# One low part of a weight form in each second pair: a subtraction on VectorE instead of an accumulating DMA

## The chip, the cores and the metric

The kernel runs on one core of one Trainium2 chip. The metric is the device time of one execution in microseconds; lower is better. A core has TensorE for matrix products, VectorE (DVE in the profile) and ScalarE (ACT) for elementwise work, GpSimd (POOL) and SyncE (SP), and 16 DMA engines that all queues share.

## The reference

A two-layer encoder over 512 frames of 1024 features. Layer 0 mixes with an mLSTM, layer 1 with a gated MLP; each layer is wrapped by two half-step SwiGLU feed-forward networks and ends with a gated embedding. The change lies in the feed-forward network, which is run four times:

```python
def swiglu_ffn(x, w_gu, w_d):
    g, u = jnp.split(x @ w_gu, 2, axis=-1)
    return (jax.nn.silu(g) * u) @ w_d
...
    x = layer_norm(DN_ALPHA * x + 0.5 * swiglu_ffn(x, ffn1_wgu[i], ffn1_wd[i]), ln_g[i, 0], ln_b[i, 0])
```

x is 512 x 1024, w_gu 1024 x 5632 and w_d 2816 x 1024, all in float32.

## The kernel before, in words

**Split operands.** A float32 product is made of three matmuls on parts of reduced precision: high by high, low by high, high by low (lines 387 to 389). So every weight tile becomes two tiles before TensorE may use it: the high part, `whi`, a copy on ScalarE (line 274), and the low part, `wlo`, which is the tile minus its high part.

**Two ways to make a low part.** Either VectorE subtracts (line 283 at once, or line 289 later: then it stands in a list, `pending`, until `lows` is called); or ScalarE writes the negative of the tile's reduced copy into `wlo` (line 280) and GpSimd issues a DMA that adds the tile onto it (line 281). For the second way `by_dma` must hold the form.

**Seven products for eight.** The hidden width of 2816 is 22 blocks of 128, taken in chunks of 2, 4, 4, 4, 4, 4 blocks (`FFN_CHUNKS`). In the last two chunks, 4 and 5, the product that goes up, x times w_gu, is made pair by pair of blocks: gate and up columns, each in two halves of the inner dimension, are four quarters of w_gu of 128 x 1024 elements (512 KB each, loaded by SyncE into halves of three `wbox` buffers, or whole buffers of 1 MB called `wraw` once the chunk is over). From them `up_forms` builds seven forms in place, by additions and subtractions on VectorE (lines 139 and 140 for the third, 147 and 148 for the fifth), and TensorE makes seven products instead of eight. `UP_BY_DMA = (1, 3, 4, 5, 6)` says which of the seven forms, counted from 0, get their low part from a DMA; forms 0 and 2 get it from VectorE.

**Order of the work.** A chunk of four blocks has two pairs, so 14 products up, here called u0 to u13 (u0 to u6 of the first pair, u7 to u13 of the second), and seven products down for the chunk before, d0 to d6. `ffn_weights` writes the order: u0 u1 d0 u2 u3 d1 u4 u5 d2 u6 u7 d3 u8 u9 d4 u10 u11 d5 u12 u13 d6. The fifth form of the second pair, form 4 there, belongs to u11. A product up is 24 matmuls of 256 columns, one down 12 of 512 columns. Two products up and one down are called a block of work below.

**Buffers and who waits.** The high and low tiles of the products up have four buffers each (`W_BUFS`), so the form of u11 is made after u7 has been given back, while TensorE is at d3. In a step of `up_products` the order in the program is: the product's matmuls, the taking of its result, the low part of the hidden activations' form (`finish_form`, line 943, tile `flo`), the pending low parts of weights (`W.lows`, line 1143), then new forms (`W.release`). VectorE and ScalarE run strictly in that order. The form of u11 frees a quarter of w_gu when its low part is made (`done`, line 287): by DMA that is when the accumulating DMA has landed, since it reads the quarter. The next load into that place on SyncE's queue waits for it, and everything behind it on that queue too.

The tiles' names in the profile: `ups` the result of a product up, `gps` of one down, `fhi` and `flo` the parts of the hidden activations' form, `us` and `xt` partial sums, `wquarter` the quarters of w_d.

Of the kernel before, what the change touches and what calls it, by code (L numbers as in the profile page):

```python
# [17 lines left out]
P = 128  # L18
# [5 lines left out]
HID = 2816  # L24
# [19 lines left out]
EXTRA = 2  # L44
PLE_EXTRA = 3
UP_BY_DMA = (1, 3, 4, 5, 6)


class Weights:
# [75 lines left out]
        self.after.update({t2: (made[0][1],), t1: (made[1][1], t2)})  # L125
        return [(kind, js, make) for js, make in made]

    def up_forms(self, j11, j12, j21, j22):

        vec, raws = self.nc.vector, self.raws  # L130

        def a11():
            return raws[j11], ()

        def a12():
            return raws[j12], ()

        def s2():
            vec.tensor_add(raws[j21], raws[j21], raws[j22])
            vec.tensor_sub(raws[j11], raws[j21], raws[j11])  # L140
            return raws[j11], ()

        def s1():
            return raws[j21], (j21,)

        def s3():
            vec.tensor_sub(raws[j12], raws[j12], raws[j11])
            vec.tensor_sub(raws[j11], raws[j22], raws[j11])
            return raws[j11], (j11,)

        def s4():
            return raws[j12], (j12,)

        def a22():
            return raws[j22], (j22,)

        made = [((j11,), a11), ((j12,), a12), ((j21, j22), s2), ((), s1), ((), s3), ((), s4), ((), a22)]
        for _, make in made:
            self.in_place.add(make)
        self.after.update({s2: (a11,), s3: (a12, s2)})  # L160
        self.by_dma.update(made[r][1] for r in UP_BY_DMA)
        return [("main", js, make) for js, make in made]

    def spare(self, kind):
# [192 lines left out]
def hybrid_trunk(ctx: ExitStack, tc, x, p, ln_g, ln_b, ffn1_wgu, ffn1_wd, ffn2_wgu, ffn2_wd,  # L357
# [87 lines left out]
    def kp(w):  # L445
        return w.rearrange("(kb p) c -> p kb c", p=P)
# [4 lines left out]
    def add_pairs(w, a0, b0):  # L451

        W.add((w_cols(w, a0), cols2), (w_cols(w, b0), cols2))
# [4 lines left out]
    def add_rows(w, kb, n, kind="main"):  # L458
        for k in range(0, n, 2):
            W.add((kp(w)[:, kb + k:kb + k + 2, :], rows2), kind=kinds_of(kind, k))  # L460
# [14 lines left out]
    def ffn_weights(wgu, wd, name, ple=False):  # L475
        starts = [sum(FFN_CHUNKS[:c]) for c in range(LAST + 1)]

        def forms(c):
            m = FFN_CHUNKS[c] // 2

            def quarter(i, j):
                k = starts[c] + m * i
                return kp(wd)[:, k:k + m, j * 512:(j + 1) * 512]
            loads = [W.add_load(quarter(i, j), n, name) for i, j, n in ((0, 0, 2), (0, 1, 1), (1, 1, 1), (1, 0, 2))]
            return W.forms("rows", *((j, slice(None)) for j in loads))

        first = len(W.order)
        for at in range(starts[UP_FROM]):
            if at == 0 or at == starts[UP_FROM] - 1:
                W.add(*((kp(wgu)[:, :, c0:c0 + P], [slice(None)]) for c0 in (at * P, HID + at * P)))  # L490
            elif at % 2:
                add_pairs(wgu, at * P, HID + at * P)
        tiles = W.order[first:]
        del W.order[first:]
        for c, n in enumerate(FFN_CHUNKS):
            down_w = deque(forms(c - 1) if c else ())
            if c >= UP_FROM:
                products = []
                for b in range(starts[c], starts[c] + n, 2):
                    products += W.up_forms(*(W.add_load(kp(wgu)[:, k:k + 4, c0:c0 + 2 * P], 1, "box")  # L500
                                             for c0 in (b * P, HID + b * P) for k in (0, 4)))
                for s, product in enumerate(products):
                    W.order.append(product)
                    if s % 2:
                        W.order.append(down_w.popleft())
                continue
            for i in range(2 * n):
                W.order.append(tiles[2 * starts[c] + i])
                if down_w:
                    W.order.append(down_w.popleft())  # L510
        if ple:
            W.add_hook("rows", lambda hi, lo: turn_p.pop()(hi, lo))
        add_rows(wd, starts[LAST], 4, ["rowsx", "rows", "main", "main"] if ple else ["main", "rows", "rowsx", "rows"])
# [74 lines left out]
    def ple_weights(i):  # L588
        add_rows(ple_wp[i], 0, 2)
        add_wide(ple_wg[i], 0, ["extra", "extra", "extra", "main"])  # L590
        add_wide(ple_wg[i], 512, ["rows", "rows", "rowsx", "rows2"])

    ffn_weights(ffn1_wgu[0], ffn1_wd[0], (0, 0))
    ml_weights()
    ffn_weights(ffn2_wgu[0], ffn2_wd[0], (0, 2), True)
    ple_weights(0)
    ffn_weights(ffn1_wgu[1], ffn1_wd[1], (1, 0))
    gm_weights()
    ffn_weights(ffn2_wgu[1], ffn2_wd[1], (1, 2), True)
# [1350 lines left out]
```

## Time and profile before

| | |
|---|---|
| median of 3 runs | 2241.99 us (2235.75 to 2245.25) |
| the profiled execution's own time | 2245.95 us |
| its span on the core | 2244.2 us |
| mean granted TensorE clock | 0.992 |
| busy: TensorE, VectorE, ScalarE, GpSimd | 98%, 75%, 48%, 8% |
| accumulating DMAs of 512 KB from `wbox` tiles | 80 |
| HBM read | 224.58 MB, 101 GB/s over the span |

Busy shares are of the span. An engine's row in the timeline has its start, its duration, the line, the tiles as written <- read, and in square brackets how long the engine had been idle before it and what ended that. A row of the windows has the stretch, its length, then for each engine its busy time with the count of instructions, then the granted clock, the busy share of the DMA engines and their GB/s. A row of DMA issues has the number of issues, the size and the median time from issue to landing in us.

### The profile page before, as it was taken

The numbers are of one execution on the slowest core, as the hardware profiler recorded it, in microseconds if no ns is written. First come the engines' busy times: TensorE is split into PE (matmuls) and PEld (weight loads), VectorE is DVE, ScalarE is ACT, GpSimd is POOL, SyncE is SP. The second block draws the span as 40 slices with busy tenths as digits, with TensorE's granted clock in tenths as the row PEclk, the third lists the DMA queues.
The fourth block names the chain that finished last, engine by engine and source line by source line (L and its number), as shares of the span: only waits on it lengthen the run. The fifth ranks groups of instructions, "written<-read, shape, count | busy, mean of one in ns | idle before, by whom it ended". The sixth has DMA issues, their size and how long they took to land.

```text
span 2244.2 us, 29572 instructions
## 1 busy us (share of the span) xinstructions
PE 2205.9 (98%) x11669; PEld 1900.9 (85%) x11669; DVE 1675.5 (75%) x2436; ACT 1076.6 (48%) x1508; POOL 172.5 (8%) x215
## 2 busy tenths in 40 slices
PE   9999999999999999999999999999999999999998
PEld 8888988888888888888888888898888888888987
DVE  5668877786767776697786768886788767678887
ACT  3334655464646433356444334665345553336642
POOL 1000110111101100001000000110001100001100
PEclk9999999999999999999999999999999999999999
DMA  6334864456847432267632334764437743336651
GB/s 194 105 99 132 185 147 138 104 137 136 155 127 150 132 127 91 89 153 171 173 127 67 113 103 121 189 137 137 141 93 140 162 140 113 103 113 139 156 176 57
DMA packets 218355, 295.71 MB, mean 132 GB/s; under 512 B 7604, under 2 KB 162356, under 8 KB 218216
## 3 DMA queue, kind: packets, MB, share of 16 engines
q1 hardware_dynamic: 168592, 211.83, 29.3%
q0 software_dynamic: 43008, 67.30, 18.5%
q10 hardware_dynamic: 6616, 14.69, 1.9%
q8 instruction: 92, 1.51, 0.3%
q14 instruction: 47, 0.39, 0.0%
HBM read 224.58 MB, written 2.11 MB: 101 GB/s over the span
## 4 chain that ended last, share of the span: by engine, by line
PE 76%; DVE 11%; ACT 5%; DMA 4%; issue 3%; POOL 0%; SPq 0%; DVEq 0%; POOLq 0%; ACTq 0%
PE fps L387 7%; PE fps L388 7%; PE fps L389 7%; PE gps L387 5%; PE gps L388 5%; PE gps L389 5%; DMA wlo<-wbox 3%; PE dps L388 2%; PE dps L389 2%; PE dps L387 2%; DVE wlo L289 2%; PE ups L389 2%; PE ups L387 2%; PE ups L388 2%; ACT whi L274 1%
## 5 line engine op out<-in xcount | busy, mean ns | idle before, releaser
L274 ACT ACTIVATE whi<-wraw 128x1024 fp32r<-128x1024 f32 (+1 forms) x276 | 283.2, 1045 | 95.5 <-DVE wraw L118 22.5
L387 PE MATMUL fps<-xh,whi 128*128 128x512 f32 x800 | 311.4, 389 | 0.0
L388 PE MATMUL fps<-xl,whi 128*128 128x512 f32 x800 | 311.2, 389 | 0.0
L389 PE MATMUL fps<-xh,wlo 128*128 128x512 f32 x800 | 311.2, 389 | 0.0
L283 DVE TENSOR_TENSOR wlo<-wraw,whi 128x1024 fp32r<-128x1024 f32 (+1 forms) x204 | 245.0, 1215 | 48.8 <-ACT whi L274 48.0
L387 PE MATMUL gps<-whi,fhi 128*128 128x512 f32 x644 | 252.8, 393 | 0.0
L388 PE MATMUL gps<-wlo,fhi 128*128 128x512 f32 x644 | 252.3, 392 | 0.0
L389 PE MATMUL gps<-whi,flo 128*128 128x512 f32 x644 | 251.8, 391 | 0.0
L274 ACT ACTIVATE whi<-wquarter 128x1024 fp32r<-128x1024 f32 (+1 forms) x140 | 135.7, 969 | 213.1 <-PE gps L389 136.4
L283 DVE TENSOR_TENSOR wlo<-wquarter,whi 128x1024 fp32r<-128x1024 f32 (+1 forms) x92 | 97.6, 1061 | 151.9 <-ACT whi L274 151.9
L762 DVE TENSOR_TENSOR xt<-xt,gps 128x512 f32<-128x512 f32 x302 | 193.5, 679 | 5.5 <-PE gps L389 5.5
L274 ACT ACTIVATE whi<-wbox 128x1024 fp32r<-128x1024 f32 x112 | 117.9, 1052 | 131.5 <-DVE wbox L140 63.6
L389 PEld LDWEIGHTS fps<-xh,wlo 128*128 128x128 f32 x800 | 150.2, 188 | 31.5
L387 PEld LDWEIGHTS fps<-xh,whi 128*128 128x128 f32 x800 | 150.2, 188 | 31.0
L388 PEld LDWEIGHTS fps<-xl,whi 128*128 128x128 f32 x800 | 150.2, 188 | 30.9
L389 PE MATMUL ups<-xh,wlo 128*128 128x256 f32 x512 | 150.5, 294 | 22.1 <-DMA wlo<-wbox 22.1
L281 POOL DMA_DIRECT2D wlo<-wbox x80 | 68.0, 850 | 1170.6 <-ACT wlo L280 968.9
L387 PE MATMUL ups<-xh,whi 128*128 128x256 f32 x512 | 149.5, 292 | 0.4
L388 PE MATMUL ups<-xl,whi 128*128 128x256 f32 x512 | 149.0, 291 | 0.0
L389 PEld LDWEIGHTS gps<-whi,flo 128*128 128x128 f32 x644 | 121.3, 188 | 26.5
L387 PEld LDWEIGHTS gps<-whi,fhi 128*128 128x128 f32 x644 | 122.0, 189 | 24.0
L388 PEld LDWEIGHTS gps<-wlo,fhi 128*128 128x128 f32 x644 | 121.7, 189 | 23.7
(365 smaller groups left out, 5203.3 us busy)
## 6 DMA issues: line engine op xcount, KB each, us to landing
wraw<-in_ffn_wgu_dram SPq DMA_DIRECT2D x47, 1024.0 KB, 6.7
wlo<-wbox POOLq DMA_DIRECT2D x80, 512.0 KB, 5.9
wquarter<-in_ffn_wd_dram SPq DMA_DIRECT2D x64, 512.0 KB, 3.8
wbox<-in_ffn_wgu_dram SPq DMA_DIRECT2D x64, 512.0 KB, 5.5
wraw<-in_ml_w_in_dram SPq DMA_DIRECT2D x24, 1024.0 KB, 5.6
wlo<-wraw POOLq DMA_DIRECT2D x48, 512.0 KB, 6.4
wraw<-in_gm_w_in_dram SPq DMA_DIRECT2D x15, 1024.0 KB, 5.7
wraw<-in_ffn_wgu_dram SPq DMA_DIRECT2D x17, 512.0 KB, 4.9
```

The lines of the kernel that those rows point to most:

```text
L274: self.nc.scalar.activation(hi[:, s], src[:, s], AF.Copy)
L281: self.nc.gpsimd.dma_start(lo[:, s], src[:, s], accum_op=OP.add)
L283: self.nc.vector.tensor_sub(lo[:, s], src[:, s], hi[:, s].bitcast(F32))
L289: self.nc.vector.tensor_sub(lo, src, hi.bitcast(F32))
L387: mm(ps, st[0], mv[0], start=start, stop=False, skip_group_check=more)
L388: mm(ps, st[0], mv[1], start=False, stop=False, skip_group_check=more)
L389: mm(ps, st[1], mv[0], start=False, stop=stop, skip_group_check=more)
L762: vec.tensor_add(dst, dst, ps)
```

## The change

Form 4 of the second pair of each chunk leaves the set of forms whose low part is made by DMA. With four feed-forward networks, two such chunks each and one such form in each, that is eight forms in the program. For each of them ScalarE's negative copy (line 280) and GpSimd's accumulating DMA (line 281) go, and VectorE gets one subtraction of 128 x 1024 elements (line 289), through the list of pending low parts. The first pair is as before, and so is everything else.

```diff
 UP_BY_DMA = (1, 3, 4, 5, 6)
+UP_BY_DMA_2 = (1, 3, 5, 6)
...
-    def up_forms(self, j11, j12, j21, j22):
+    def up_forms(self, j11, j12, j21, j22, by_dma=UP_BY_DMA):
...
-        self.by_dma.update(made[r][1] for r in UP_BY_DMA)
+        self.by_dma.update(made[r][1] for r in by_dma)
...
                     products += W.up_forms(*(W.add_load(kp(wgu)[:, k:k + 4, c0:c0 + 2 * P], 1, "box")
-                                             for c0 in (b * P, HID + b * P) for k in (0, 4)))
+                                             for c0 in (b * P, HID + b * P) for k in (0, 4)),
+                                            by_dma=UP_BY_DMA if b == starts[c] else UP_BY_DMA_2)
```

The program's lines are one to three further down after the change (289 becomes 290). The rows below are of the first feed-forward network, chunk 4, around the form of u11; its parts are `whi_2108` and `wlo_2109`.

VectorE before, from the taking of u8's result on (`us_2106`):

```order
L1087 TENSOR_TENSOR us_2106<-us_2106,ups_2132 128x512 [waits PE_49,Activation_49]
L943 TENSOR_TENSOR flo_2130<-h_1296,fhi_2129 128x512 [waits Activation_49]
L289 TENSOR_TENSOR wlo_2127<-wquarter_1466,whi_2126 128x1024
L762 TENSOR_TENSOR xt_86<-xt_86,gps_1839 128x512 [waits DVE_49,PE_49]
L762 TENSOR_TENSOR xt_86<-xt_86,gps_1840 128x512 [waits DVE_49,PE_49]
L943 TENSOR_TENSOR flo_2219<-h_1296,fhi_2218 128x512 [waits Activation_49]
```

VectorE with the change, at the same place:

```order
L1089 TENSOR_TENSOR us_2106<-us_2106,ups_2129 128x512 [waits PE_49,Activation_49]
L945 TENSOR_TENSOR flo_2127<-h_1296,fhi_2126 128x512 [waits Activation_49]
L290 TENSOR_TENSOR wlo_2109<-wbox_1595,whi_2108 128x1024 [waits DVE_49]
L290 TENSOR_TENSOR wlo_2124<-wquarter_1466,whi_2123 128x1024
L764 TENSOR_TENSOR xt_86<-xt_86,gps_1839 128x512 [waits DVE_49,PE_49]
L764 TENSOR_TENSOR xt_86<-xt_86,gps_1840 128x512 [waits DVE_49,PE_49]
L945 TENSOR_TENSOR flo_2218<-h_1296,fhi_2217 128x512 [waits Activation_49]
```

The new subtraction stands behind `flo`, which waits for ScalarE, and ahead of the low part of d5's weights.

ScalarE before, from the high part of u11's form on:

```order
L274 ACTIVATE whi_2108<-wbox_1595 128x1024 [waits DVE_49,Activation_49]
L280 ACTIVATE wlo_2109<-wbox_1595 128x1024 [waits DMASW5_49]
L274 ACTIVATE whi_2126<-wquarter_1466 128x1024 [waits PE_49,Activation_49]
L940 ACTIVATE fhi_2129<-h_1296 128x512 [waits Activation_49]
L274 ACTIVATE whi_2164<-wbox_1595 128x1024 [waits PE_49,Activation_49]
L280 ACTIVATE wlo_2165<-wbox_1595 128x1024 [waits DMASW1_49,PE_49]
```

ScalarE with the change:

```order
L275 ACTIVATE whi_2108<-wbox_1595 128x1024 [waits DVE_49,Activation_49]
L275 ACTIVATE whi_2123<-wquarter_1466 128x1024 [waits PE_49,Activation_49]
L942 ACTIVATE fhi_2126<-h_1296 128x512 [waits Activation_49]
L275 ACTIVATE whi_2163<-wbox_1595 128x1024 [waits PE_49,Activation_49]
L281 ACTIVATE wlo_2164<-wbox_1595 128x1024 [waits DMASW1_49,PE_49]
```

One copy is gone; `fhi`, for which VectorE's `flo` waits, and the two copies for u12 (`wlo_2164`) move up by one place.

SyncE's queue of loads before; DMASW3 is the landing of u11's accumulating DMA, DMASW4 that of u12's:

```order
L238 DMA wbox_1534<-in_ffn1_wgu_dram 128x4x256 [waits DMAHW3_49,DMASW2_49,Activation_49]
L238 DMA wbox_1595<-in_ffn1_wgu_dram 128x4x256 [waits DMASW3_49,DMAHW4_49,DVE_49,Activation_49]
L238 DMA wquarter_2162<-in_ffn1_wd_dram 128x2x512 [waits DMAHW5_49,DVE_49,Activation_49]
L238 DMA wbox_1595<-in_ffn1_wgu_dram 128x4x256 [waits DMAHW6_49,DMASW4_49,Activation_49]
L238 DMA wbox_1472<-in_ffn1_wgu_dram 128x4x256 [waits DMAHW7_49,DMASW5_49,Activation_49]
```

SyncE's queue with the change, where DMASW3 is now u12's landing and DMASW4 that of u13's:

```order
L239 DMA wbox_1534<-in_ffn1_wgu_dram 128x4x256 [waits DMAHW3_49,DMASW2_49,Activation_49]
L239 DMA wbox_1595<-in_ffn1_wgu_dram 128x4x256 [waits DMAHW4_49,DVE_49,Activation_49]
L239 DMA wquarter_2161<-in_ffn1_wd_dram 128x2x512 [waits DMAHW5_49,DVE_49,Activation_49]
L239 DMA wbox_1595<-in_ffn1_wgu_dram 128x4x256 [waits DMAHW6_49,DMASW3_49,Activation_49]
L239 DMA wbox_1472<-in_ffn1_wgu_dram 128x4x256 [waits DMAHW7_49,DMASW4_49,Activation_49]
```

The loads are the same in the same order; the second of them waits for VectorE where it waited for u11's DMA. In chunk 5 the same holds for the second of the two 1 MB loads of w_d. TensorE's instructions stand as before, but u11's first matmul with the low part waits for VectorE and not for a DMA.

## The prediction

> **What bounds the kernel now.** I read the page's busy times first, then TensorE's waits, then the place of each wait, then the engines around one of them.
>
> ```profile
> PE 2205.9 (98%) x11669; PEld 1900.9 (85%) x11669; DVE 1675.5 (75%) x2436; ACT 1076.6 (48%) x1508; POOL 172.5 (8%) x215
> ```
>
> TensorE is busy for 98% of the span, so a gain can only come from its idle time or from its clock. Who ends its idle time, in the waits of TensorE (total us, times, longest):
>
> ```profile
> PE ups L389 <- DMA wlo<-wbox: 23.5, 9, 4.3
> PE dps L388 <- DVE wlo L289: 1.8, 2, 0.9
> ```
>
> Nine waits for an accumulating DMA make nearly all of it. The timeline of TensorE shows where they are; here the first and the largest, with neighbours, and the ninth:
>
> ```profile
> 259.12 0.28 PE L389 MATMUL ups<-t,wlo 128*128 128x256 f32 x1
> ...
> 259.36 0.28 PE L388 MATMUL ups<-xl,whi 128*128 128x256 f32 x1
> 261.67 0.58 PE L389 MATMUL ups<-xh,wlo 128*128 128x256 f32 x1 [2.02 <-DMA wlo<-wbox]
> 262.04 0.41 PE L387 MATMUL ups<-xh,whi 128*128 128x256 f32 x1
> 262.26 0.41 PE L388 MATMUL ups<-xl,whi 128*128 128x256 f32 x1
> ...
> 327.43 0.58 PE L389 MATMUL ups<-xh,wlo 128*128 128x256 f32 x1 [4.27 <-DMA wlo<-wbox]
> ...
> 1517.90 0.38 PE L389 MATMUL ups<-t_f,wlo 128*128 128x256 f32 x1 [1.38 <-DMA wlo<-wbox]
> ```
>
> The matmul that waits is the third of its product, the first that needs the low part. Product u10 (right operand `t`) ends just before, so the waiting product is u11, whose low part the change moves. The same place comes eight times, in chunks 4 and 5 of the four networks; the ninth wait, at 1517.90, is u13's (right operand `t_f`). After the wait the matmuls follow each other at 0.22 us (262.04 to 262.26) where it was 0.12 before it (259.12 to 259.24 and on to 259.36). The windows give the clock for that, and the price of each whole block u10 u11 d5. The first row is a block without a wait, the next eight are those with u11, and the last row is the stretch just behind the first wait; columns are length, TensorE's busy time and count, granted clock, DMA share, GB/s (in the last row more engines stand between).
>
> ```profile
> 247.89:256.39 8.50, 8.50 (x62) 1.00 0.61 132
> 256.39:268.58 12.19, 10.17 (x61) 0.86 1.02 233
> 319.54:335.50 15.96, 11.59 (x62) 0.79 0.89 227
> 1020.28:1035.07 14.79, 11.42 (x62) 0.77 1.03 258
> 1086.03:1101.62 15.59, 11.27 (x69) 0.89 1.01 249
> 1439.13:1451.92 12.79, 10.23 (x61) 0.87 0.99 237
> 1502.88:1513.25 10.37, 8.99 (x62) 1.00 1.02 263
> 2069.64:2080.22 10.58, 8.73 (x61) 1.00 1.02 233
> 2131.18:2145.17 13.99, 11.33 (x70) 0.88 1.04 264
> ```
>
> ```profile
> 261.67:264.95 3.28, 3.28 (x15) 3.28 (x16) 1.83 (x2) 2.20 (x4) 0.45 (x1) 0.50 1.06 214
> ```
>
> The reader is to see that the eight blocks take 10.4 to 16.0 us for work that takes 8.50, and that in six of them the granted clock is under 0.9: behind the stalls TensorE runs at half its clock for some microseconds. Two blocks, at 1086 and 2131, hold eight transposes more, 0.8 us until the next block (2145.17 less 2144.38):
>
> ```profile
> 2144.38 1.03 PE L1817 MATMUL ptp<-ident,pt 128*128 128x128 f32 x8
> ```
>
> So the excess is 3.69 + 7.46 + 6.29 + 6.29 + 4.29 + 1.87 + 2.08 + 4.69 = 36.7 us. Of it 23.5 - 1.4 = 22.1 us is idle time, and about 14.6 the half clock and the restart.
>
> **What the change removes, adds and moves.** Around the first u11 the other engines do this (ScalarE, then VectorE, then GpSimd):
>
> ```profile
> 252.71 1.06 ACT L274 ACTIVATE whi<-wbox 128x1024 fp32r<-128x1024 f32 x1 [3.11 <-DVE wbox L148]
> 253.68 1.04 ACT L280 ACTIVATE wlo<-wbox 128x1024 fp32r<-128x1024 f32 x1
> ...
> 255.57 0.61 ACT L940 ACTIVATE fhi<-h 128x512 fp32r<-128x512 f32 x1
> ...
> 257.04 1.04 ACT L280 ACTIVATE wlo<-wbox 128x1024 fp32r<-128x1024 f32 x1
> ```
>
> ```profile
> 256.22 0.69 DVE L943 TENSOR_TENSOR flo<-h,fhi 128x512 fp32r<-128x512 f32 x1 [1.81 <-ACT fhi L940]
> 256.83 1.22 DVE L289 TENSOR_TENSOR wlo<-wquarter,whi 128x1024 fp32r<-128x1024 f32 x1
> ...
> 262.48 0.69 DVE L943 TENSOR_TENSOR flo<-h,fhi 128x512 fp32r<-128x512 f32 x1 [3.23 <-ACT fhi L940]
> ```
>
> ```profile
> 258.38 0.84 POOL L281 DMA_DIRECT2D wlo<-wbox  x1 [2.52 <-ACT wlo L280]
> ```
>
> Removed at each place: ScalarE's copy at 253.68, which holds its queue for 0.95 us (to the next start), an issue on GpSimd, and a DMA of 512 KB. All of ScalarE's work behind it up to 262 runs without a pause, so `fhi` ends at 255.24 and u12's copies end near 257.1. Added: one subtraction of 1.22 us on VectorE, 9.8 us in all eight. It starts when `flo` is done: `flo` moves up with `fhi` to 255.27, the subtraction runs from 255.88 to 257.10. TensorE wants the low part at 261.67 - 2.02 = 259.65. So it is there 2.5 us early, and the whole wait goes. Behind it stand the low part of d5's weights (now to 258.3, needed when d5 begins near 262.4) and two sums; VectorE's pause of 3.23 us ahead of 262.48 hides the 1.22. If that cover were gone, the later low parts would come 1.22 us later in each of the eight.
>
> In chunk 5 the same steps lie elsewhere in time (VectorE, GpSimd, SyncE):
>
> ```profile
> 319.73 0.69 DVE L943 TENSOR_TENSOR flo<-h,fhi 128x512 fp32r<-128x512 f32 x1 [1.81 <-ACT fhi L940]
> ```
>
> ```profile
> 321.90 0.84 POOL L281 DMA_DIRECT2D wlo<-wbox  x1 [2.52 <-ACT wlo L280]
> ```
>
> ```profile
> 316.97 10.97 SPq L238 DMA_DIRECT2D wraw<-in_ffn_wd_dram  x2
> ```
>
> `flo` moves to 318.78, the subtraction ends at 320.6, needed at 327.43 - 4.27 = 323.16: again 2.5 us early. The row of SyncE holds two loads of 1 MB, the second issued at its end, 327.6, when u11's DMA had landed. With the change that load waits only for the subtraction, so it goes at about 320.7, just ahead of u12's accumulating DMA (321.90 less 0.95, so 320.95).
>
> What is late next is therefore u12. Its low part is wanted one block after u10 began: 319.54 + 8.50 + 0.24 = 328.28, which is 7.3 us after its issue. In chunk 4: 256.39 + 8.74 = 265.13, with the issue at 257.43, 7.7 us. How long such a DMA takes, from the rows of issues, each with one issue in its window: alone (at 277); u11's in chunk 5 beside the first 1 MB load (at 318, 1085, 1501, 2130); u13's right behind a 1 MB load (at 1508):
>
> ```profile
> wlo<-wbox POOLq DMA_DIRECT2D x1, 512.0 KB, 4.5
> ```
>
> ```profile
> wlo<-wbox POOLq DMA_DIRECT2D x1, 512.0 KB, 8.9
> ```
>
> ```profile
> wlo<-wbox POOLq DMA_DIRECT2D x1, 512.0 KB, 8.8
> ```
>
> ```profile
> wlo<-wbox POOLq DMA_DIRECT2D x1, 512.0 KB, 5.9
> ```
>
> ```profile
> wlo<-wbox POOLq DMA_DIRECT2D x1, 512.0 KB, 7.1
> ```
>
> ```profile
> wlo<-wbox POOLq DMA_DIRECT2D x1, 512.0 KB, 9.7
> ```
>
> The five beside a load have a mean of 8.1 us. u12 in chunk 5 will stand as they did, so I put its wait at 8.1 - 7.3, about 0.75 us, and 3.0 in four; the ends are 0 (4.5 alone) and 2.4 each (9.7). In chunk 4 the early load has half the size and there are 7.7 us, so I put 0 there.
>
> A stretch of DMA traffic, 318 to 330 in forty parts, shows how the queue shares out: the 1 MB load at about 400 GB/s first, then the accumulating DMAs at about 210.
>
> ```profile
> GB/s 177 109 82 287 328 396 437 410 396 410 423 205 205 191 218 164 177 232 218 219 232 218 218 205 218 218 218 219 205 218 218 191 177 191 137 218 219 55 232 396
> ```
>
> By the Trainium skill, page "DMA: Bandwidth & Descriptors", section "Queues, rings and completion order", each DMA engine goes round robin between the rings that have work, packet by packet. By that rule u12's DMA would not stand behind the load but share with it; it would land after some 4.5 + 2.4 = 6.9 us (an estimate: 512 KB more at 210 GB/s), with no wait, and the sum below would be 3 lower. The row shows the load going ahead of the DMAs, not sharing.
>
> u13's wait of 1.38 us at 1517.90 comes from a DMA of 9.7 us right behind the second 1 MB load; that load goes earlier now, so I take this wait off, and count u12's instead.
>
> The sum against the profiled execution: 2245.95 - 36.7 - 1.4 + 3.0 = 2210.9, so 2211. That execution lies 4.0 us above the median of the runs, 2241.99; the runs spread over 9.5 us, as stalls with a half clock behind them would make them. Against the median the gain is 31 us, 1.4%.
>
> **The rivals.** *The stall moves to u12 (chunk 5).* The early 1 MB load makes each of its four DMAs take 9.7 us: a wait of 2.4, and with the half clock about 4 as in the block at 1439 (4.29, with a wait of the same kind). Four times 4 instead of 3.0: 2224. For it: three of five rows are over 8.8. Against: without u11's DMA there is 512 KB less in the queue ahead of it. If u12 in chunk 4 also took 9.7, a wait of 2.0, four blocks would cost as the first one does, 3.7 each, 15 more: 2239, *no change to speak of*, from landings of about 9.5 on everywhere.
>
> *The half clock is not the stalls'.* The rows show the clock low behind waits of 2.02 and more and full in the blocks at 1502 and 2069; if the clock fell for another reason than the wait, it would stay low. Then the three longest waits take their part along (7.46, 6.29, 6.29 less their idling, length less busy time of those rows without the transposes: 4.3, 3.4 and 4.3; 8 us), and 6 us of the others' 14.6 stay: 2211 + 6, about 2218. The Trainium skill, page "TensorE: Matmul & The Clock Gate", section "What's actually happening", has the clock halved after an idle window of about 3.4 us. The row at 261.67 speaks against it as a minimum: 2.02 us of idling was enough.
>
> *Slower: VectorE's wait takes the DMA's place.* The subtraction stands behind `flo`, and that behind ScalarE's `fhi`. If `fhi` were as late as the next one is, the subtraction would run where the row 262.48 stands, from 263.08 to 264.30, and TensorE would wait 4.65 us instead of 2.02. Blocks with waits of over 4 us cost 6.3 to 7.5, so eight cost 55 instead of 36.7: 2264. It decides when the subtraction ends later than 261.67. Against it: `fhi` stands only behind copies that run without a pause, and ends at 255.24.
>
> **How the numbers follow.** The forecast, u11's stalls gone with their half clock and small waits at u12: 0.72, 2211. The stall at u12 in chunk 5: 0.12, 2224. The clock's part stays: 0.08, 2218. The stall at u12 everywhere: 0.05, 2239. VectorE's wait: 0.03, 2264. Faster by over 0.5% (11 us, about what a measurement of this kernel can tell from no change) are the first three, 0.92; within it 0.05; slower 0.03. The range reaches from 2205 (no wait at all is 2208, and 3 us for the spread of runs) to 2226 (the second case, with 2 us of that spread).
>
> **What would show it.** In the profile after: the waits of TensorE have no u11 in them, and blocks u10 u11 d5 take 8.5 us at a clock of 1.00; the subtraction stands at about 255.9 and 319.4; the second 1 MB load is issued about 7 us earlier. Wrong would be a wait of u11 for VectorE, waits of u12 over 2 us with the half clock behind them, or a low clock without a wait ahead of it.

## The result and the profile after

| | before | with the change |
|---|---|---|
| median | 2242.47 us (2235.75 to 2245.25, 4 runs) | 2213.66 us (2212.3 to 2214.41, 4 runs) |
| profiled execution | 2245.95 us | 2213.68 us |
| its span | 2244.2 us | 2212.0 us |
| granted TensorE clock | 0.992 | 0.999 |

The ratio is 0.9875, with an interval of 0.9853 to 0.9898: 1.25% faster, or 28.8 us by the medians. 2211 us was forecast, 31 us under the median on record then.

The busy row of the page, and TensorE's waits (total us, times, longest):

```profile
PE 2192.9 (99%) x11669; PEld 1889.2 (85%) x11669; DVE 1684.5 (76%) x2444; ACT 1069.6 (48%) x1500; POOL 166.1 (8%) x207
```

```profile
PE ups L390 <- DMA wlo<-wbox: 4.9, 9, 1.0
PE dps L389 <- DVE wlo L290: 1.8, 2, 0.9
```

The waits for accumulating DMAs fell from 23.5 to 4.9 us, and none is longer than 1.0. TensorE's busy time fell too, by 13.0 us, though its instructions are the same: that is the half clock that is gone (eight windows of 3.41 us before, and none now ahead of the program's last matmuls). The windows of the blocks, first u10 u11 d5, then u12 u13 d6, show both (length, busy time of TensorE, its weight loads, VectorE, ScalarE, GpSimd, granted clock, DMA share, GB/s):

```profile
255.42:263.90 8.48, 8.48 (x62) 7.98 (x60) 6.37 (x8) 8.46 (x11) 1.69 (x2) 1.00 0.97 258
263.90:273.14 9.24, 8.75 (x61) 8.06 (x60) 9.12 (x12) 5.28 (x6) 1.15 (x2) 1.00 0.85 215
315.60:324.08 8.48, 8.48 (x62) 7.98 (x60) 6.38 (x8) 6.92 (x10) 1.69 (x2) 1.00 0.95 256
324.08:333.72 9.64, 8.76 (x62) 8.07 (x60) 6.52 (x9) 3.27 (x4) 0.00 (x0) 1.00 1.02 301
...
1018.48:1028.05 9.57, 9.01 (x62) 8.11 (x60) 9.35 (x12) 5.17 (x6) 1.15 (x2) 1.00 0.88 209
...
1079.78:1089.63 9.85, 8.84 (x64) 8.14 (x62) 6.51 (x10) 3.82 (x6) 0.00 (x0) 1.00 0.88 272
...
1426.67:1435.65 8.98, 8.74 (x61) 8.05 (x60) 8.86 (x12) 5.28 (x6) 1.14 (x2) 1.00 0.94 238
...
1486.59:1497.01 10.42, 9.02 (x62) 8.12 (x60) 6.64 (x9) 3.78 (x5) 0.00 (x0) 1.00 0.96 295
...
2051.76:2060.79 9.03, 8.75 (x62) 8.06 (x60) 8.91 (x12) 5.29 (x6) 1.16 (x2) 1.00 0.87 221
...
2112.51:2121.44 8.93, 8.84 (x63) 8.16 (x62) 6.50 (x10) 3.83 (x6) 0.00 (x0) 1.00 0.92 282
```

Less the 0.8 us of transposes in two of them, all eight blocks with u11 take 8.47 or 8.48 us, where they took 10.4 to 16.0. The eight blocks behind them, with u12 and u13, take 7.5 us more than their work: 8.50 is a block without waits, and 8.58 in the two at 1079.78 and 2112.51, so 0.74 + 1.14 + 1.07 + 1.27 + 0.48 + 1.92 + 0.53 + 0.35. Before, only one of these eight was longer, by 1.63.

VectorE around the new subtraction, in chunk 4 and then in chunk 5 of the first network:

```profile
254.33 0.69 DVE L945 TENSOR_TENSOR flo<-h,fhi 128x512 fp32r<-128x512 f32 x1 [0.86 <-ACT fhi L942]
254.94 1.22 DVE L290 TENSOR_TENSOR wlo<-wbox,whi 128x1024 fp32r<-128x1024 f32 x1
```

```profile
314.86 0.69 DVE L945 TENSOR_TENSOR flo<-h,fhi 128x512 fp32r<-128x512 f32 x1 [0.86 <-ACT fhi L942]
315.46 1.22 DVE L290 TENSOR_TENSOR wlo<-wbox,whi 128x1024 fp32r<-128x1024 f32 x1
```

This run is 0.97 us ahead of the one before by the start of that part (u10 begins at 255.42, where it began at 256.39), so the subtraction stands within 0.1 us of the forecast 255.88. It ends at 256.16; u11 wants the low part one product and two matmuls into its block, at about 255.42 + 3.24 = 258.66.

What is left, in TensorE's timeline: the first wait of each kind, u13 in chunk 4 (right operand `t_f`) and u12 in chunk 5.

```profile
267.66 0.39 PE L390 MATMUL ups<-t_f,wlo 128*128 128x256 f32 x1 [0.49 <-DMA wlo<-wbox]
...
325.35 0.39 PE L390 MATMUL ups<-xh,wlo 128*128 128x256 f32 x1 [0.88 <-DMA wlo<-wbox]
```

SyncE's two loads of 1 MB in chunk 5, and the issue rows of u12's DMA there (issued at 317.02), of u12's in chunk 4 (256.49) and of u13's in chunk 4 (259.38):

```profile
313.06 4.07 SPq L239 DMA_DIRECT2D wraw<-in_ffn_wd_dram  x2
```

```profile
wlo<-wbox POOLq DMA_DIRECT2D x1, 512.0 KB, 8.3
...
wlo<-wbox POOLq DMA_DIRECT2D x1, 512.0 KB, 6.4
...
wlo<-wbox POOLq DMA_DIRECT2D x1, 512.0 KB, 8.2
```

The second load's issue runs from 316.76 to 317.13, a quarter of a microsecond ahead of u12's DMA, as forecast; that DMA then takes 8.3 us. What moved in the meantime, by queue (packets, MB, share of the 16 DMA engines; q1 has SyncE's loads, q0 GpSimd's DMAs), first from 317.0 to 321.5, then from 321.5 to 325.3:

```profile
q1 hardware_dynamic: 252, 0.97, 86.8%
...
q0 software_dynamic: 182, 0.68, 90.2%
q1 hardware_dynamic: 59, 0.18, 13.6%
```

Up to 321.5 nothing of u12's DMA moves: its first packet starts 4.9 us after its issue, when the load is nearly through. In the other three networks that is 5.3, 4.9 and 4.8 us; in `ladder` below, where that load comes behind it, 1.4 us.

### The profile page after: what moved, and what is told of

Read it like the earlier page. It is cut to its first block, busy times and chain, and to the rows that moved or that the text cites. A ratio compares the mean times of both kernels' runs of the same rounds, so it can differ in the third digit from the quotient of the medians.

```text
span 2212.0 us, 29545 instructions
## 1 busy us (share of the span) xinstructions
PE 2192.9 (99%) x11669; PEld 1889.2 (85%) x11669; DVE 1684.5 (76%) x2444; ACT 1069.6 (48%) x1500; POOL 166.1 (8%) x207
## 4 chain that ended last, share of the span: by engine, by line
PE 76%; DVE 10%; issue 5%; ACT 5%; DMA 3%; SPq 0%; POOL 0%; DVEq 0%; ACTq 0%; POOLq 0%
PE fps L388 7%; PE fps L389 7%; PE fps L390 7%; PE gps L390 6%; PE gps L388 6%; PE gps L389 6%; DMA wlo<-wbox 3%; PE dps L389 2%; PE dps L390 2%; PE dps L388 2%; DVE wlo L290 2%; ACT whi L275 1%; PE ups L390 1%; PE vps L388 1%; PE zps L388 1%
## 5 line engine op out<-in xcount | busy, mean ns | idle before, releaser
L390 PE MATMUL ups<-xh,wlo 128*128 128x256 f32 x512 | 145.4, 284 | 3.3 <-DMA wlo<-wbox 3.2
L282 POOL DMA_DIRECT2D wlo<-wbox x72 | 61.3, 851 | 1160.1 <-ACT wlo L281 991.0
L388 PE MATMUL ups<-xh,whi 128*128 128x256 f32 x512 | 144.8, 283 | 0.0
```

What stands on the lines that cost most here:

```text
L282: self.nc.gpsimd.dma_start(lo[:, s], src[:, s], accum_op=OP.add)
L388: mm(ps, st[0], mv[0], start=start, stop=False, skip_group_check=more)
L390: mm(ps, st[1], mv[0], start=False, stop=stop, skip_group_check=more)
```

## The experiments

The theory: the gain is the late DMA of u11, the stall that it made, and the half clock that the stall brought. What remains is u12's and u13's DMAs running beside loads. Rivals: fewer DMAs and copies help wherever they are; ScalarE's copy was the cost; the half clock has another cause. The first four kernels ran on one chip, where the kernel before took 2239.88 us, the last four on another, where it took 2240.40 us; each ratio is against the kernel before on the same chip.

**The same edit in the wrong pair** (`first_pair`).

```diff
-                                            by_dma=UP_BY_DMA if b == starts[c] else UP_BY_DMA_2)
+                                            by_dma=UP_BY_DMA_2 if b == starts[c] else UP_BY_DMA)
```

> The same edit, made in the wrong pair: u4 (the fifth form of the first pair) gets its low part by VectorE, u11 by the accumulating DMA again. As many accumulating DMAs and copies of ScalarE are taken away as in the change; only the place differs. My theory (the gain is u11's late DMA and what its stall brings after it): the stalls of 1.3 to 6 us ahead of u11 and the half clock behind them come back in the eight places, so about 2242 us, within 4 us of the kernel before. Rival (the gain comes from fewer DMAs, 4.2 MB less on the queues, and fewer copies of ScalarE, wherever they are): about 2214 us, as the change.

Measured: 2236.62 us, ratio 0.9982 (0.9971 to 0.9992). Its waits, and its longest:

```profile
PE ups L390 <- DMA wlo<-wbox: 18.2, 9, 4.4
```

```profile
1085.12 0.58 PE L390 MATMUL ups<-xh,wlo 128*128 128x256 f32 x1 [4.36 <-DMA wlo<-wbox]
```

The stalls ahead of u11 are back, and with them all but 3 us of the gain, though as many DMAs and copies are gone as in the change. So the place makes the gain, and the number of DMAs and copies some 3 us of it at most. The waits are 5.3 us fewer in sum than before; why, this run doesn't tell.

**ScalarE's copy stays** (`keep_copy`): the copy is made for u11 and overwritten.

```diff
+                elif make in self.copied:
+                    self.nc.scalar.activation(lo[:, s], src[:, s], AF.Copy, scale=-1.0)
```

> The change, but ScalarE's copy with the sign turned, which went out with the DMA, stays for u11 and is overwritten by VectorE's subtraction. My theory (the gain is the DMA that u11 no longer waits for; the copy itself was not on the path): u11 is still on time, TensorE has no wait ahead of it; ScalarE's copies for u12 and u13 come some 0.95 us later, so their DMAs start later and the small waits at u12 and u13 (7.5 us over the eight places after the change) grow by at most 8 x 0.95 us: 2214 to 2222 us. Rival (it is ScalarE's 0.95 us that moved everything): the gain mostly gone, over 2235 us.

Measured: 2218.94 us, ratio 0.9902 (0.9887 to 0.9917). The copy, and TensorE's waits:

```profile
252.92 1.04 ACT L287 ACTIVATE wlo<-wbox 128x1024 fp32r<-128x1024 f32 x1
```

```profile
PE ups L395 <- DMA wlo<-wbox: 8.2, 10, 1.5
```

The blocks with u11 take 8.47 us in chunk 4 and 8.83 in chunk 5, and all waits for the DMAs together grew by 3.3 us. I had expected nothing ahead of u11, and in chunk 5 that was wrong: u11's product goes to the buffer (`bank[0]`) from which ScalarE takes u9's result, and with the copy in front ScalarE takes it later. So u11 begins 3.1 us after u10 there, as in the kernel before; in the change it begins 2.85 us after u10. ScalarE's copy is worth about 4 us of the 25 on this chip (2239.88 less 2215.10); the rest went with the DMA. This run does not part the transfer itself from GpSimd's issue and from the load that waited for its landing; `late_free` below puts that load off again in chunk 4, and u11 has no wait there.

**The change again** (`after_again`), beside these two.

> The change itself, beside the others on one chip: 2214 us by every theory, with waits of TensorE ahead of u12 and u13 of up to 1 us each in the two chunks of each feed-forward network.

Measured: 2215.10 us, ratio 0.9883 (0.9869 to 0.9898). TensorE waits for accumulating DMAs eight times, 4.8 us in all and 1.1 at most.

**The early load put off** (`late_free`): u11's quarter is freed only with u12's form.

```diff
-            return raws[j11], (j11,)
+            return raws[j11], (() if by_dma is UP_BY_DMA_2 else (j11,))
...
-            return raws[j12], (j12,)
+            return raws[j12], ((j12, j11) if by_dma is UP_BY_DMA_2 else (j12,))
```

> The change, but u11's forming no longer frees its quarter of the weights at once: the quarter is freed with u12's, so that the 1 MB load that the change had pulled ahead of u12's DMA waits until after it again. My theory (u12's DMA is late because that load is served first): u12's DMA lands in 5 to 6.5 us where it took 8.3 us in the second of the two chunks, the waits ahead of u12 there (0.4 to 1 us each, with u12's part 3.5 us or so of the 7.5 us left) go, 2209 to 2212 us. Rival (the DMA is slow from the other traffic and the load's place doesn't matter): 2213 to 2215 us. A second rival (the load, put off, makes a later form late): slower than 2216 us.

Measured: 2219.50 us, ratio 0.9906 (0.9889 to 0.9923): 4 us slower than the change. TensorE's waits; the issue rows in chunk 4 of the first network, of u12's DMA, of the load that was put off, and of u13's DMA; and the wait that follows:

```profile
PE ups L390 <- DMA wlo<-wbox: 10.5, 8, 2.5
```

```profile
wlo<-wbox POOLq DMA_DIRECT2D x1, 512.0 KB, 5.7
...
wbox<-in_ffn_wgu_dram SPq DMA_DIRECT2D x1, 512.0 KB, 11.2
...
wlo<-wbox POOLq DMA_DIRECT2D x1, 512.0 KB, 9.8
```

```profile
269.27 0.39 PE L390 MATMUL ups<-t_f,wlo 128*128 128x256 f32 x1 [2.01 <-DMA wlo<-wbox]
```

I was wrong here in two ways. In chunk 4 the load's place does matter for u12's DMA: 5.6 to 5.7 us in all four networks, where the change has 6.4, 8.1, 7.4 and 7.2. But the load then runs beside u13's DMA, which lands after 8.1 to 10.3 us, and u13 was the late one there already, as `u12_too` and `u13_too` show below. So the second rival's range came true, through u13's DMA. In chunk 5 the edit did not move the load: the second 1 MB load is issued 1.15 us after u10's start in both kernels. u12's DMA was no earlier there, 8.6 us in three networks and 9.9 in the first, where TensorE waited 2.46 us for it; why it took longer there is not shown. The three longest waits of this trace (2.01, 2.46 and 2.49 us) each have a half clock of 3.41 us behind them, which is part of the loss. What u12's DMA takes with that load behind it can be read in `ladder`, where the repeated subtractions put the load off: 4.5 to 5.0 us in all four chunks 5. So the theory of the load's place holds for u12, but this edit did not put it to use.

**Stalls made by VectorE alone** (`ladder`): u11's subtraction is repeated, over the same tile.

```diff
+MORE = [4, 3, 4, 4, 4, 3, 4, 4]
...
+                for _ in range(self.more.get(make, 0)):
+                    self.nc.vector.tensor_sub(lo, src, hi.bitcast(F32))
                 if late:
                     self.nc.vector.tensor_sub(lo, src, hi.bitcast(F32))
```

> The change, with u11's subtraction on VectorE repeated 3 or 4 more times over the same tile (3 in chunk 5 of the first and third feed-forward network, 4 in the other six places), so that u11's low part is late by VectorE alone and no DMA is the cause: at 1.22 us each it should come 1.5 us late with 3 and 2.4 (chunk 4) to 2.7 us late (chunk 5) with 4. The traces so far show the half clock in windows of 3.41 us on a fixed grid, behind windows that held 1.62 us or more of idle TensorE and behind none that held 1.53 us or less. My theory (the half clock is a consequence of the stall, whoever makes it): stalls that put over 1.6 us into one window are followed by a half clock of 3.4 us, those of 1.5 us, and those that the grid cuts in two smaller parts, by none; with 18 us of stalls less the 7.5 us of waits at u12 and u13 that fall into them, and some 1.7 us for each half clock, 2224 to 2236 us. Rival A (the half clock comes with the late DMA, as heavy traffic or load): the clock stays at 1.0 throughout. Rival B (the Trainium skill's page on TensorE, Matmul and The Clock Gate, puts the step at an idle window of about 3.4 us): the clock stays at 1.0 too, since no stall is that long.

Measured: 2234.88 us in one execution. TensorE's waits; VectorE at the first place; and two of the eight waits:

```profile
PE ups L396 <- DVE wlo L296: 19.3, 8, 2.9
```

```profile
254.53 5.00 DVE L294 TENSOR_TENSOR wlo<-wbox,whi 128x1024 fp32r<-128x1024 f32 x4
259.56 1.23 DVE L296 TENSOR_TENSOR wlo<-wbox,whi 128x1024 fp32r<-128x1024 f32 x1
```

```profile
260.85 0.58 PE L396 MATMUL ups<-xh,wlo 128*128 128x256 f32 x1 [2.55 <-DVE wlo L296]
...
1019.49 0.39 PE L396 MATMUL ups<-xh,wlo 128*128 128x256 f32 x1 [2.54 <-DVE wlo L296]
```

No DMA is waited for any more, and five of the eight stalls are followed by a half clock of 3.41 us. Rival A and rival B both had none. Stalls of one length, 2.55 and 2.54 us, were followed by a half clock at 260.85 and not at 1019.49. The windows of TensorE around these two, and around the 1.65 us stall of chunk 5, on the grid on which the clock changes (length, busy time, granted clock, DMA share, GB/s):

```profile
256.85:260.26 3.41, 1.45 (x13) 1.00 0.81 154
260.26:263.68 3.42, 2.83 (x13) 0.50 1.00 175
1014.61:1018.02 3.41, 2.34 (x20) 1.00 0.84 199
1018.02:1021.43 3.41, 1.94 (x16) 1.00 0.99 172
1021.43:1024.85 3.42, 3.42 (x20) 1.00 0.89 234
```

```profile
321.70:325.12 3.42, 1.77 (x15) 1.00 0.95 164
325.12:328.53 3.41, 3.41 (x21) 1.00 1.06 233
```

At 256.85 the window held 1.96 us of idling, and the next runs at half clock. At 1014.61 the grid cut the same stall into 1.07 and 1.47, and the clock stayed. The two blocks u10 u11 d5 are 12.52 and 11.27 us long, so this half clock cost 1.25 us beside its stall. One thing I had not expected: 1.65 us, all in one window, brought no half clock, where I had put the step at 1.6.

**u12 by VectorE as well** (`u12_too`), **u13** (`u13_too`), **both** (`u12_u13_too`).

```diff
-UP_BY_DMA_2 = (1, 3, 5, 6)
+UP_BY_DMA_2 = (1, 3, 6)      # u12_too
+UP_BY_DMA_2 = (1, 3, 5)      # u13_too
+UP_BY_DMA_2 = (1, 3)         # u12_u13_too
```

> The change made for u12 as well: its low part by VectorE too, so that only u13 (and the second and fourth form) of the second pair keep the DMA. My theory (what is left, 7.5 us, is u12 and u13 waiting for DMAs that run beside a load): u12's waits go, and u13's DMA starts about a copy of ScalarE (0.95 us) earlier and with no other DMA of its kind in front of it, so its waits shrink too: 2206 to 2209 us. Rival (loads are pulled ahead again, now ahead of u13's DMA, and the wait moves to u13): 2211 to 2215 us. Second rival (VectorE, which has one more subtraction of 1.22 us and the two copies into place, becomes late for u12): over 2216 us.

> The change made for u13 as well, not for u12: u13's waits go, u12's stay, and more of the wait shows at u12 than before only if its DMA gets later. My theory: u12's DMA is unchanged beside its load (8.3 us in the second chunk), so about 4 to 5 us of the 7.5 us stay: 2209 to 2212 us. Rival (u13's DMA shared the queue with u12's and held it up): u12 lands earlier too, 2206 to 2208 us. Second rival (VectorE late): over 2216 us.

> The change made for u11, u12 and u13: only the second and fourth form of the second pair keep the DMA. My theory: no DMA is waited for in the second pair any more, VectorE's two more subtractions (2.4 us) fit into the 8.5 us of a block of work, and the 7.5 us of waits that the change left go: 2206 to 2208 us. Rival (VectorE becomes the late one, at u13 or at the first forms of the next chunk, since its work bunches at the chunk's end): 2210 to 2225 us, with waits of TensorE for VectorE's subtraction in place of the DMA's.

Measured: `u12_too` 2207.93 us, ratio 0.9852 (0.9836 to 0.9869); `u13_too` 2211.61 us, 0.9869 (0.9854 to 0.9884); `u12_u13_too` 2206.40 us, 0.9846 (0.9831 to 0.9860). For each in that order: TensorE's waits, and the windows of blocks u12 u13 d6 in chunks 4 and 5 of the first network (in the last kernel the block of u11 ahead of it, in chunk 4 alone).

```profile
PE ups L390 <- DMA wlo<-wbox: 1.9, 2, 1.0
```

```profile
263.71:273.45 9.74, 8.76 (x61) 8.07 (x60) 8.56 (x11) 5.17 (x6) 0.83 (x2) 1.00 0.69 163
...
324.39:332.89 8.50, 8.50 (x62) 8.01 (x60) 5.62 (x8) 3.27 (x4) 0.00 (x0) 1.00 0.91 303
```

```profile
PE ups L390 <- DMA wlo<-wbox: 3.1, 3, 1.6
```

```profile
263.82:272.32 8.50, 8.50 (x61) 8.01 (x60) 8.38 (x11) 5.28 (x6) 0.83 (x2) 1.00 0.75 188
323.25:333.00 9.75, 8.77 (x61) 8.07 (x60) 6.70 (x9) 3.27 (x4) 0.00 (x0) 1.00 0.93 286
```

```profile
PE dps L389 <- DVE wlo L290: 1.8, 2, 0.9
```

```profile
255.16:263.63 8.47, 8.47 (x61) 7.98 (x60) 8.47 (x10) 6.64 (x9) 0.31 (x1) 1.00 0.89 282
263.63:272.13 8.50, 8.50 (x61) 8.01 (x60) 8.38 (x11) 5.28 (x6) 0.84 (x2) 1.00 0.40 87
```

With u12 by VectorE the rest waits only in chunk 4, for u13; with u13 by VectorE only in chunk 5, for u12. So u12's DMA is the late one in chunk 5 and u13's in chunk 4, for the most part. In `u12_too` u13's waits in chunk 4 did not shrink as I had expected: its DMA starts 0.96 us earlier after u10, but takes 8.7 to 9.7 us instead of 8.0 to 8.4, beside a load of w_gu that now goes 3.0 us after u10's start; two waits of 1.0 us are left. With both, no wait for an accumulating DMA is left, and the time is 2206.4: 8.7 us under the change run again, on the other chip (where the kernel before was 0.5 us slower), near the 7.5 us that the blocks had left. This version beats both kernels. It has used up VectorE: 8.47 busy of 8.47 us in the block of u11, 8.38 of 8.50 in the next, so in chunk 4 of this network there is no room for another low part.

## Why the prediction was right

**The term of u11, 36.7 us, was right**: its eight blocks are 36.9 us shorter. `first_pair` shows that the place makes the gain, and `keep_copy` that nearly all of it went with the DMA. Four times 0.36 us of it, in chunk 5, were not the DMA's: there ScalarE's copy itself held u11 up, which the prediction did not see.

**VectorE in time** was right: the subtraction stands where it was put. `ladder` measures the reserve: four more subtractions delay the low part by 259.56 - 254.53 = 5.03 us and make a wait of 2.55, so the reserve is 2.5 us in chunk 4, as worked out. In chunk 5 three more (3.77 us) make 1.65, so it is 2.1 and not 2.5: the prediction took the time at which TensorE wants the low part from the kernel before, where the copy made it 0.36 us later. The rival "VectorE's wait takes the DMA's place" did not come, but `ladder` confirms its mechanism: eight such waits of 1.65 to 2.9 us make the span 21.2 us longer (2233.2 against 2212.0).

**The early load** was right in time and place, and so was its direction for u12: in chunk 5 u12's DMA took 8.3, 9.3, 8.4 and 8.4 us, where 8.1 was put. The round robin of the Trainium skill, page "DMA: Bandwidth & Descriptors", section "Queues, rings and completion order", by which the prediction had 6.9 us and no wait, is not what this trace shows in any of the four: the DMA stood behind the load, as the rows by queue show. Why it did is not shown.

**The step that was mis-sized is what comes next.** For u12 in chunk 5 there were 3.0 us, for chunk 4 none, and 1.4 us of u13's old wait were taken off. The blocks show 4.7 us in chunk 5 (1.14 + 1.27 + 1.92 + 0.35), against 1.6 there before, and 2.8 in chunk 4 (0.74 + 1.07 + 0.48 + 0.53). The sum of this step is 7.5 - 1.6 = 5.9 us more than before, where 3.0 - 1.4 = 1.6 was forecast. Two things failed in it. First, in chunk 4 I priced only u12's DMA against its 7.7 us of time; u13's, which follows and also runs beside the loads (8.2 us in the row above), I did not price at all (and in the second network u12's own took 8.1 us and was waited for, 0.36 us). Second, a wait of 0.88 makes its block 1.14 longer: each stall costs some 0.26 us beside the idling, and I had left that out for the small ones. With these, 2245.95 - 36.9 + 5.9 gives 2214.9; the start of the program up to chunk 4 was 0.97 shorter in this run, 2214.0, and 2213.68 was measured.

**The rival "stall moves to u12"** had the right place and too high a price: no wait was over 1.01 us (1.14 when the change ran again), and none brought a half clock.

**The half clock** is a consequence of the stall: it went with the stalls, came back with them in `first_pair`, and came without any late DMA in `ladder`. By the Trainium skill, page "TensorE: Matmul & The Clock Gate", section "What's actually happening", the halving follows an idle window of about 3.4 us. The grid of 3.41 us agrees with that page's window; that all of it has to be idle does not, since 1.96 us of idling in one was enough.

## What to carry to other kernels

Price a transfer that stands between two engines by its landing beside the traffic of that very moment (here 6.4 to 9.3 us, against 4.5 alone), and when one is taken away, do the same sum for each transfer behind it, not only for the next. An engine that is busy for 76% of the span can still take the work in the stage that waits, if the row of windows shows it room there; the same row shows when the room is used up. A stall of about 2 us costs more than its idling, since the clock may be halved behind it, so several short waits were cheaper here than one as long as their sum, although each cost some 0.26 us beside its idling.

## What the runs showed of the hardware

The granted clock changes on a fixed grid of 3.41 us: in `first_pair` the six places ahead of the program's end at which it fell (322.961, 1019.28, 1084.133, 1500.559, 2067.172 and 2132.025 us) lie whole multiples of 3.4133 us apart. What goes with it is the idle time inside one window of that grid. Over the traces of before, of the change and of the experiments, behind the program's start, the window after was at half clock whenever a window at full clock held 1.89 us or more of idle time, and never when it held 1.53 us or less. In between the cases differ: 1.62 us in `first_pair` had a half clock behind it, and 1.65 in `ladder` at 321.70 above had none. Nor had the windows with 1.61, 1.77, 1.80 and 1.83 us in which the last matmuls of `ladder`, `late_free`, `u12_too` and `first_pair` ended, though only idling followed them. So the idle time alone does not decide between 1.6 and 1.8 us, and what does is open. The windows of `first_pair` with 1.53 (at 258.11) and 1.62 us idle, and those behind them (length, busy time, granted clock, DMA share, GB/s):

```profile
258.11:261.52 3.41, 1.88 (x16) 1.00 1.07 211
261.52:264.93 3.41, 3.41 (x23) 1.00 1.05 200
319.55:322.96 3.41, 1.79 (x13) 1.00 1.06 210
322.96:326.37 3.41, 3.41 (x17) 0.50 1.01 256
```

So a stall of 2.5 us costs a half clock or not by where the grid happens to cut it. The grid lies elsewhere from one execution to another: counted back in steps of 3.4133 us from the first fall (261.544 us in before, 260.263 in `ladder`, 269.533 in `late_free`), its first line is 2.1, 0.85 and 3.3 us behind the span's start. That fits with the runs of before being spread over 9.5 us and those of the change over 2.1 us.
